# Encoder block on one core: where the first splits of the down projection and of its last unit are written, and how the final norm is multiplied

## The chip, the cores and the metric

The kernel runs on 1 core of one Trainium2 chip. The metric is the device time of one execution in microseconds; the median of three executions of the kernel before is 2689.52 us (2682.81 to 2689.66). The profile is of one more execution.

## The reference

The program computes one encoder layer (512 tokens, 2048 features, two attention mixers, then a SwiGLU feed-forward network of 5632 hidden features) and a final RMS norm. Only the end of it matters here:

```python
h2 = rms_norm(x, norm2_w[l]) * (1.0 + sc2) + sh2
ff = (jax.nn.silu(h2 @ w_ffn_gate[l]) * (h2 @ w_ffn_up[l])) @ w_ffn_down[l]
x = x + g2 * ff
return rms_norm(x, final_w)
```

with `rms_norm(x, w) = x * rsqrt(mean(x*x) + eps) * w`. All is float32.

## The kernel before, in words

**Arithmetic.** A float32 matmul is made of three: every operand is split into a high part (`S.activation(hi, src, AF.Copy)`, line 144, on ScalarE, called ACT in the profile) and a low part (`V.tensor_sub(lo, src, hi)`, line 145, on VectorE, DVE), both of type float32r, and `mm3` (lines 152 to 154) issues high*high, high*low and low*high into one PSUM bank on TensorE (PE).

**Order.** The order of the instructions on each engine is fixed when the kernel is built. A scheduler takes them by their place in the program (blocks under `tc.high_priority()` first) and by when it believes them ready, and puts each behind those already placed on its engine or DMA queue. At run time an engine works its list in order and waits at an instruction whose semaphores have not come; what stands behind it waits too. The DMA queues are SP's (`nc.sync`, nearly all loads and stores), ACT's (`nc.scalar`) and POOL's (`nc.gpsimd`, GpSimd); the kernel before issues no DMA from POOL. Tiles are handed out of pools. Pools lie on two stacks (left and right); a new pool's tiles are placed by the scheduler only after the pools under which it lies have been released, in program order; at run time a tile waits only for the old tiles that it overlaps (`reuse_waits="tile"`).

**Buffers.** `raw_tile` gives one of 5 staging buffers of 512 KB (128 x 1024 f32), shared by weights (`raw`) and by features read back (`ffr`). `wtile` gives one of 5 pairs of split weight buffers (`whi`, `wlo`). PSUM has 8 banks: four tagged `mm`, two `S`, one `T`, one `Y`.

**Gate and up products.** For each of 11 units `n` (512 hidden features) `group7` makes the gate and the up product by a seven-product scheme: 4 steps of 84 matmuls over the normalised features `hx` (pools `f_x` left, `f3` right), on seven banks (`BANK`: four `mm`, two `S`, `Y`). `wforms` loads the weights of a step and builds two sums of blocks in the tiles `ta` (2 buffers) and `tb`. At the end lines 839 to 846, under high priority, combine the banks into a tile `c` (3 buffers, pool `c_p`, right). Then ACT takes SiLU of the gate's tile, DVE multiplies the two (line 914, two instructions) and a DMA stores the product to `ff_d[n]` in HBM (line 915): from SP, and for the last unit from ACT.

**Down projection.** `FF` gives the hidden features of units back: for each pair of two 128-feature slices it loads half of `ff_d[u]` (line 959) and splits it into tiles `f0h`, `f0l`, `f1h`, ... of pool `p_f`. `form2` runs 512 output columns: per step of two slices one `wsplit` of `w_down`, then for each slice 3 matmuls into each of four `mm` banks (one for each 128 tokens, index `i`), then `pump()`, which takes one item off the list `later`; at the end `residual` multiplies each bank by the gate row `g2` (line 725, DVE) and adds it to `x2` (line 726, here on POOL). Units 0 to 4 run first, for the four column blocks `cc`, then units 5 to 9. `later` holds `reload`: the loads of `g2` (four DMAs, 1 MB) and of the four 1 MB tiles `xr` (the residual stream `x2`), in pool `p_c`.

**Last unit.** Unit 10's features are split into pool `p_fl`; its weights (four column blocks, each in two halves `k`) are split into tiles `w0h`, `w0l` to `w3h`, `w3l` of pool `p_l`, which lies where `p_f` was. Then, for each 128 tokens `i` and each `cc`, 12 matmuls into an `mm` bank, `residual` on DVE with a square on ACT (line 241, with its sum), and after the fourth `cc` `row_rstd` (lines 245 and 230 to 236: seven small DVE instructions and a square root on ACT), and line 999, which multiplies four times in one instruction by the row factor and by `final_w` (`fw`), each followed by a store of 256 KB from SP.

Of the kernel before, what the change touches and what calls it, by code (L numbers as in the profile page):

```python
# [13 lines left out]
F32 = mybir.dt.float32  # L14
# [5 lines left out]
P = 128  # L20
D = 2048
# [76 lines left out]
def encoder_block(ctx: ExitStack, tc, xp, xT, c, w_ada, ada1_w, b_ada, norm1_w, w_in, q_norm_w, k_norm_w, tb,  # L98
# [24 lines left out]
    def raw_tile(name="raw"):  # L123
        return buffer("raw", [P, 1024], F32, wbufs["raw"], name)
# [6 lines left out]
    def bank(tag):  # L131
        return ps.tile([P, 512], F32, tag=tag, name=tag, bufs={"mm": 4, "S": 2, "T": 1, "Y": 1}[tag])
# [10 lines left out]
    def split(hi, lo, src, eng=V):  # L143
        S.activation(hi, src, AF.Copy)  # L144
        eng.tensor_sub(lo, src, hi)  # L145
# [63 lines left out]
    def form2(w, c0, xs, evac, r0=0, eng=V, tiles=range(NT)):  # L209

        n = len(xs)
        banks = {i: bank("mm") for i in tiles}
        for k0 in range(0, n, 2):
            m = min(2, n - k0)
            hi, lo = wsplit(w, r0 + k0, m, c0, 512, eng)
            for kk in range(m):
                xh, xl = xs[k0 + kk]
                for i in tiles:
                    sl = slice(i * P, (i + 1) * P)
                    mm3(banks[i], xh[:, sl], xl[:, sl], hi[:, kk], lo[:, kk], k0 + kk == 0, k0 + kk == n - 1)  # L220
            pump()
        for i in tiles:
            evac(i, banks[i])
# [125 lines left out]
    def rows(dst, src):  # L349
        for q in range(4):  # L350
            nc.sync.dma_start(dst[:, q * 512:(q + 1) * 512], src[q].partition_broadcast(P).rearrange("p o d -> p (o d)"))
# [406 lines left out]
    def form_pool(name, side):  # L758
        return tc.alloc_tile_pool(name=name, bufs=1, side=side, reuse_waits="tile")
# [62 lines left out]
    def group7(wsrc, xs, order, dst):  # L822

        bk = {r: bank(BANK[r]) for r in ORDER}
        for n, s in enumerate(order):
            w = wsrc(s)
            for r in ORDER:
                (wh, wl), (xh, xl) = w[r], xs[s][r]
                for q in range(2):
                    for c in range(2):  # L830
                        o = bk[r][:, c * 256:(c + 1) * 256]
                        cs = slice(c * P, (c + 1) * P)
                        first, last = n == 0 and q == 0 and c == 0, n == len(order) - 1 and q == 1
                        mm3(o, wh[:, q, cs], wl[:, q, cs], xh[:, q], xl[:, q], first, last, skip_group_check=True)
        p = {r: b.rearrange("p (c n) -> p c n", c=2) for r, b in bk.items()}
        (d11, d12), (d21, d22) = dst
        with tc.high_priority():
            p1 = io.tile([P, 512], F32, tag="io", name="p1").rearrange("p (c n) -> p c n", c=2)
            S.activation(p1, p[1], AF.Copy)
            V.tensor_add(d11, p[2], p1)  # L840
            V.tensor_add(d21, p[6], p1)
            V.tensor_add(d12, p[5], d21)
            V.tensor_add(d12, p[3], d12)
            V.tensor_add(d21, p[7], d21)
            V.tensor_add(d22, p[5], d21)
            V.tensor_sub(d21, d21, p[4])
# [48 lines left out]
    def c_tile():  # L895
        c = c_p.tile([P, 2048], F32, tag="c", name="c", bufs=3)
        return c, c.rearrange("p (a t q n) -> p a t q n", a=2, t=2, q=2)

    for n in range(FU):
        cs = []  # L900
        for w in (w_gate, w_up):
            c, v = c_tile()
            cs.append(c)
            if n == 0 and w is w_gate:
                for f in range(4):
                    S.activation(v[:, f // 2, :, f % 2], banks[f].rearrange("p (t n) -> p t n", t=2), AF.Silu)
                continue
            dst = (v[:, 0, 0], v[:, 1, 0]), (v[:, 0, 1], v[:, 1, 1])
            group7(lambda s: wforms(w, 4 * s, n * 512), hx, range(SU), dst)
            if w is w_gate:  # L910
                S.activation(c, c, AF.Silu)
        for a in range(2):
            sl = slice(a * 1024, (a + 1) * 1024)
            V.tensor_mul(cs[1][:, sl], cs[1][:, sl], cs[0][:, sl])
        (nc.sync if n < FU - 1 else nc.scalar).dma_start(ff_d[n], cs[1])
    c_p.release()
    f3.release()
    for p in f_x[::-1]:
        p.release()

    wbufs["at"] = 0


    def reload(i):
        if i == 0:
            x2[:] = [p_c.tile([P, D], F32, name=f"xr{i}") for i in range(NT)]
            rows(g2, g2_d)
        nc.sync.dma_start(x2[i], x2_d[:, i])

    p_c = form_pool("p_c", "right")  # L930
    g2 = p_c.tile([P, D], F32, name="g2")
    later.append(lambda: None)
    later.extend(functools.partial(reload, i) for i in range(NT))
    p_fl = form_pool("p_fl", "left")
    p_f = form_pool("p_f", "left")

    class Tokens:

        def __init__(self, t):
            self.t = t  # L940
# [4 lines left out]

    class FF:

        def __init__(self, pool, u0, n):
            self.pool, self.u0, self.n, self.pairs = pool, u0, n, {}

        def __len__(self):
            return 4 * self.n
# [1 line left out]
        def __getitem__(self, k):  # L954
            j, q = divmod(k, 2)
            if j not in self.pairs:
                n, a = divmod(j, 2)
                raw = raw_tile("ffr")
                nc.sync.dma_start(raw, ff_d[self.u0 + n][:, a * 1024:(a + 1) * 1024])
                hl = [self.pool.tile([P, 1024], F32R, tag=f"f{j}{t}", name=f"f{j}{t}") for t in "hl"]  # L960
                split(*hl, raw)
                self.pairs[j] = hl
# [6 lines left out]
    xs = FF(p_fl, 10, 1)  # L969
    xs = [xs[k] for k in range(4)]  # L970
    p_f.release()


    f0 = 40
# [4 lines left out]
    wl = []  # L979
    for cc in range(4):  # L980
        hi, lo = pair(p_l, f"w{cc}", 4 * 512, 1)
        for k in range(0, 4, 2):
            raw, _ = unit(w_down, f0 + k, 2, cc * 512, 512)
            sl = slice(k * 512, (k + 2) * 512)
            split(hi[:, sl], lo[:, sl], raw)
        wl.append((hi, lo))
    for i in range(NT):
        sl = slice(i * P, (i + 1) * P)
        for cc in range(4):
            b = bank("mm")  # L990
            hi, lo = wl[cc]
            for k in range(4):
                ks = slice(k * 512, (k + 1) * 512)
                mm3(b, xs[k][0][:, sl], xs[k][1][:, sl], hi[:, ks], lo[:, ks], k == 0, k == 3)
            residual(cc, g2, sq3, V)(i, b)
        r = row_rstd(sq3[i])
        for cc in range(4):
            cs = slice(cc * 512, (cc + 1) * 512)
            V.scalar_tensor_tensor(x2[i][:, cs], x2[i][:, cs], r, fw[:, cs], op0=ALU.mult, op1=ALU.mult)
            nc.sync.dma_start(out[i * P:(i + 1) * P, cs], x2[i][:, cs])  # L1000
    p_l.release()
    p_fl.release()
    p_c.release()
    wq.release()
    io.release()
    wp.release()
# [30 lines left out]
```

## Time and profile before

| | |
|---|---|
| median of 3 executions | 2689.52 us |
| the profiled execution's own time | 2689.41 us |
| its span, first to last instruction | 2687.6 us |
| granted TensorE clock, mean | 0.988 |
| DVE busy | 1777.6 us, 66% of the span |
| ACT busy | 956.5 us, 36% |
| DMA read from and written to HBM | 392.11 MB and 32.52 MB |
| up product of the last unit ends, on PE | about 2184.2 us |
| down projection begins, on PE | 2191.17 us |
| last unit begins, on PE | 2628.82 us |

Times in the rows are us from the start of the span unless marked ns. A timeline row gives start, duration, engine, line, operation, output <- inputs, shape and count, and in brackets how long the engine stood idle before it and what released it. A window row gives for each engine the busy time and the number of instructions, then the granted clock of TensorE, the share of the DMA engines and GB/s.

### The profile page before, as it was taken

The page shows a single profiled execution, that of the slowest core. Times are in us where ns is not written, and L with a number is a line of the kernel's source. Part 1 is how long each engine was busy: PE and PEld are TensorE (multiplying, and loading weights), DVE is VectorE, ACT ScalarE, POOL GpSimd, SP SyncE. Part 2 cuts the span into 40 slices and gives each one's busy share as a digit, 9 for nine tenths or more (in the row PEclk, how much of TensorE's full clock was granted, in tenths as well). Part 3 has the DMA queues.
Part 4 walks back from the last instruction along what each step waited for, and adds up shares of the span by engine and source line. Part 5 has one row for each costly group of instructions (what it writes and reads, how often), then busy time and mean ns, then how long its engine had stood idle before and what let it go on. Part 6 is the DMA issues. An engine that isn't in the chain of part 4 may idle for free.

```text
span 2687.6 us, 38688 instructions
## 1 busy us (share of the span) xinstructions
PE 2608.7 (97%) x15415; PEld 2296.6 (85%) x15415; DVE 1777.6 (66%) x2508; ACT 956.5 (36%) x1292; POOL 110.3 (4%) x92
## 2 busy tenths in 40 slices
PE   6999999999999999999889999999999989999998
PEld 5888887888887878788789999999999988888886
DVE  6995687456666676653668888888888863243227
ACT  2324264223333333323544444444444442132122
POOL 0000000000000000001100000000000000010001
PEclk9999999999999999999999999999999999999999
DMA  7873424665554877774244344433444464343332
GB/s 249 278 273 106 130 83 130 213 205 170 179 179 142 265 260 248 246 240 136 84 126 126 120 132 126 126 118 119 126 127 126 126 231 146 101 146 122 100 110 86
DMA packets 247460, 427.16 MB, mean 159 GB/s; under 512 B 15984, under 2 KB 102368, under 8 KB 244720
## 3 DMA queue, kind: packets, MB, share of 16 engines
q1 hardware_dynamic: 246944, 423.59, 49.3%
q8 instruction: 121, 1.98, 0.3%
q10 hardware_dynamic: 336, 1.11, 0.1%
q14 instruction: 59, 0.48, 0.1%
HBM read 392.11 MB, written 32.52 MB: 158 GB/s over the span
## 4 chain that ended last, share of the span: by engine, by line
PE 86%; DMA 5%; DVE 5%; ACT 2%; issue 2%; POOL 0%; SPq 0%; DVEq 0%; ACTq 0%
PE mm L154 20%; PE mm L153 20%; PE mm L152 20%; PE S L152 5%; PE S L153 5%; PE S L154 5%; DMA raw<-in_w_ada 2%; PE Y L152 2%; PE Y L153 2%; PE Y L154 2%; DVE acc L303 1%; DVE wlo L145 1%; DMA g<-sga 1%; PE T L152 1%; PE T L154 1%
## 5 line engine op out<-in xcount | busy, mean ns | idle before, releaser
L145 DVE TENSOR_TENSOR wlo<-raw,whi 128x1024 fp32r<-128x1024 f32 (+1 forms) x467 | 528.5, 1135 | 459.2 <-ACT whi L144 458.3
L144 ACT ACTIVATE whi<-raw 128x1024 fp32r<-128x1024 f32 (+1 forms) x467 | 456.5, 979 | 1024.9 <-PE mm L154 420.2
L303 DVE SCALAR_TENSOR_TENSOR acc<-raw,cact,acc 128x512 f32<-128x512 f32 (+2 forms) x338 | 264.2, 788 | 118.2 <-DMA raw<-in_w_ada 111.2
L145 DVE TENSOR_TENSOR wlo<-ta,whi 128x1024 fp32r<-128x1024 f32 x84 | 102.8, 1224 | 71.5 <-ACT whi L144 71.5
L144 ACT ACTIVATE whi<-ta 128x1024 fp32r<-128x1024 f32 x84 | 89.6, 1067 | 132.0 <-PE mm L153 132.0
L144 ACT ACTIVATE whi<-tb 128x1024 fp32r<-128x1024 f32 x84 | 89.8, 1069 | 123.8 <-PE S L153 123.8
L154 PE MATMUL mm<-x1h,wlo 128*128 128x256 f32 x400 | 110.1, 276 | 1.6 <-DVE wlo L145 1.6
L152 PE MATMUL mm<-x1h,whi 128*128 128x256 f32 x400 | 110.4, 276 | 0.0
L153 PE MATMUL mm<-x1l,whi 128*128 128x256 f32 x400 | 110.3, 276 | 0.0
L145 DVE TENSOR_TENSOR wlo<-tb,whi 128x1024 fp32r<-128x1024 f32 x84 | 102.6, 1222 | 6.1 <-ACT whi L144 3.1
L152 PE MATMUL mm<-x0h,whi 128*128 128x256 f32 x368 | 102.4, 280 | 3.5 <-ACT whi L144 3.5
L154 PE MATMUL mm<-x0h,wlo 128*128 128x256 f32 x368 | 103.1, 280 | 2.6 <-DVE wlo L145 2.6
L153 PE MATMUL mm<-x0l,whi 128*128 128x256 f32 x368 | 102.6, 279 | 0.0
L726 POOL TENSOR_TENSOR xr<-xr,ro 128x512 f32<-128x512 f32 x32 | 50.1, 1599 | 1224.9 <-DVE ro L725 1224.9
L152 PE MATMUL mm<-x3h,whi 128*128 128x256 f32 x336 | 92.7, 276 | 0.0
L153 PE MATMUL mm<-x3l,whi 128*128 128x256 f32 x336 | 92.7, 276 | 0.0
L154 PE MATMUL mm<-x3h,wlo 128*128 128x256 f32 x336 | 92.7, 276 | 0.0
L152 PE MATMUL mm<-x2h,whi 128*128 128x256 f32 x336 | 92.7, 276 | 0.0
L153 PE MATMUL mm<-x2l,whi 128*128 128x256 f32 x336 | 92.7, 276 | 0.0
L154 PE MATMUL mm<-x2h,wlo 128*128 128x256 f32 x336 | 92.7, 276 | 0.0
L152 PE MATMUL S<-x2h,whi 128*128 128x256 f32 x336 | 92.7, 276 | 0.0
L153 PE MATMUL S<-x2l,whi 128*128 128x256 f32 x336 | 92.7, 276 | 0.0
(1310 smaller groups left out, 7848.0 us busy)
## 6 DMA issues: line engine op xcount, KB each, us to landing
raw<-in_w_in SPq DMA_DIRECT2D x133, 512.0 KB
raw<-in_w_gate SPq DMA_DIRECT2D x88, 512.0 KB
raw<-in_w_up SPq DMA_DIRECT2D x88, 512.0 KB
raw<-in_w_down SPq DMA_DIRECT2D x88, 512.0 KB
raw<-in_ada_w SPq DMA_DIRECT2D x64, 512.0 KB
raw<-in_w_ada SPq DMA_DIRECT2D x128, 256.0 KB
raw<-in_w_ada SPq DMA_DIRECT2D x64, 512.0 KB
raw<-in_w_out SPq DMA_DIRECT2D x40, 512.0 KB
```

What stands on the lines that cost most here:

```text
L144: S.activation(hi, src, AF.Copy)
L145: eng.tensor_sub(lo, src, hi)
L152: nc.tensor.matmul(o, lh, rh, start=start, stop=False, **kw)
L153: nc.tensor.matmul(o, lh, rl, start=False, stop=False, **kw)
L154: nc.tensor.matmul(o, ll, rh, start=False, stop=stop, **kw)
L303: V.scalar_tensor_tensor(acc, part, cact[:, k:k + 1], acc, op0=ALU.mult, op1=ALU.add)
L726: eng.tensor_add(x2[i][:, cs], x2[i][:, cs], o)
```

## The change

Five things are done.

1. A helper `ff_pair` loads and splits a pair of features into given tiles. `first_pairs`, called once after the weights of the last step of the last up product have been issued, does so for pairs 0 and 1 of unit 0: pair 0 into two tiles of tag `ta` (both buffers), pair 1 into the halves of one `c` tile. Pair 0 is used from there for all four column blocks of units 0 to 4, pair 1 for the first one only (`del xs.pairs[1]`); from the second on it is loaded and split again into `p_f`.
2. The store of the last unit's product goes from POOL's queue in place of ACT's.
3. The release of the feature pools, the new pools and the entries of `later` move into `down_pools`, called at the third pair (step `k0=4`) of the first `form2`, so that the reloads of `g2` and `xr` stand two steps later in the program.
4. The weights of the last unit's first two column blocks are loaded and split by `last_weights` into the `whi`/`wlo` buffers, ahead of the last `residual` of units 5 to 9; those of blocks 2 and 3 stay in `p_l`. The matmuls of the first 128 tokens go to banks `S`, `S`, `T`, `Y`.
5. `final_w` is multiplied into `x2` (DVE) right behind each residual; after `row_rstd` two of the four parts are multiplied by the row factor on DVE and two on ACT, and the latter are stored from ACT's queue.

```diff
+    early = {}
+    def ff_pair(unit_, a, hl):
+        raw = raw_tile("ffr")
+        nc.sync.dma_start(raw, ff_d[unit_][:, a * 1024:(a + 1) * 1024])
+        split(*hl, raw)
+        return hl
+    def first_pairs():
+        early[0] = ff_pair(0, 0, [wq.tile([P, 1024], F32R, tag="ta", name=f"e0{t}", bufs=2) for t in "hl"])
+        e1 = c_p.tile([P, 2048], F32R, tag="c", name="e1", bufs=3)
+        early[1] = ff_pair(0, 1, [e1[:, :1024], e1[:, 1024:]])
...
-            group7(lambda s: wforms(w, 4 * s, n * 512), hx, range(SU), dst)
+            def wsrc(s):
+                d = wforms(w, 4 * s, n * 512)
+                if s == SU - 1 and n == FU - 1 and w is w_up:
+                    first_pairs()
+                return d
+            group7(wsrc, hx, range(SU), dst)
...
-        (nc.sync if n < FU - 1 else nc.scalar).dma_start(ff_d[n], cs[1])
-    c_p.release()
-    f3.release()
-    for p in f_x[::-1]:
-        p.release()
+        (nc.sync if n < FU - 1 else nc.gpsimd).dma_start(ff_d[n], cs[1])
...
+    def down_pools():
+        c_p.release()
+        f3.release()
+        for p in f_x[::-1]:
+            p.release()
+        down["c"] = form_pool("p_c", "right")
+        down["g2"] = down["c"].tile([P, D], F32, name="g2")
+        later.append(lambda: None)
+        later.extend(functools.partial(reload, i) for i in range(NT))
+        down["fl"] = form_pool("p_fl", "left")
+        down["f"] = form_pool("p_f", "left")
...
             if j not in self.pairs:
+                if not down:
+                    down_pools()
                 n, a = divmod(j, 2)
...
+    def last_weights():
+        for cc in range(2):
+            us = [wsplit(w_down, f0 + k, 2, cc * 512, 512) for k in range(0, 4, 2)]
+            wl[cc] = [(hi[:, e], lo[:, e]) for hi, lo in us for e in range(2)]
     for u0 in (0, 5):
-        xs = FF(p_f, u0, 5)
+        xs = FF("f", u0, 5, early if u0 == 0 else None)
         for cc in range(4):
-            form2(w_down, cc * 512, xs, lambda i, b: residual(cc, g2, None, G)(i, b), r0=4 * u0)
+            ending = u0 == 5 and cc == 3
+            def evac(i, b):
+                if ending and i == 0:
+                    last_weights()
+                residual(cc, down["g2"], None, G)(i, b)
+            form2(w_down, cc * 512, xs, evac, r0=4 * u0)
+            if u0 == 0 and cc == 0:
+                del xs.pairs[1]
...
-    for cc in range(4):
+    for cc in range(2, 4):
         hi, lo = pair(p_l, f"w{cc}", 4 * 512, 1)
...
         for cc in range(4):
-            b = bank("mm")
+            b = bank("mm" if i else "SSTY"[cc])
...
-            residual(cc, g2, sq3, V)(i, b)
+            residual(cc, down["g2"], sq3, V)(i, b)
+            cs = slice(cc * 512, (cc + 1) * 512)
+            V.tensor_mul(x2[i][:, cs], x2[i][:, cs], fw[:, cs])
         r = row_rstd(sq3[i])
         for cc in range(4):
             cs = slice(cc * 512, (cc + 1) * 512)
-            V.scalar_tensor_tensor(x2[i][:, cs], x2[i][:, cs], r, fw[:, cs], op0=ALU.mult, op1=ALU.mult)
-            nc.sync.dma_start(out[i * P:(i + 1) * P, cs], x2[i][:, cs])
+            if cc % 2:
+                S.activation(x2[i][:, cs], x2[i][:, cs], AF.Copy, scale=r)
+            else:
+                V.tensor_scalar(x2[i][:, cs], x2[i][:, cs], r, None, op0=ALU.mult)
+            (nc.scalar if cc % 2 else nc.sync).dma_start(out[i * P:(i + 1) * P, cs], x2[i][:, cs])
```

More of the change, by code (lines that the diff above doesn't have):

```diff
@@ L914, in encoder_block @@
             V.tensor_mul(cs[1][:, sl], cs[1][:, sl], cs[0][:, sl])
-        (nc.sync if n < FU - 1 else nc.scalar).dma_start(ff_d[n], cs[1])
-    c_p.release()
-    f3.release()
-    for p in f_x[::-1]:
-        p.release()
-    wbufs["at"] = 0
+        (nc.sync if n < FU - 1 else nc.gpsimd).dma_start(ff_d[n], cs[1])
+    wbufs["at"] = 0
+    down = {}
+    def down_pools():
[9 more added lines that the diff above has]
+        down["f"] = form_pool("p_f", "left")
     def reload(i):
         if i == 0:
-            x2[:] = [p_c.tile([P, D], F32, name=f"xr{i}") for i in range(NT)]
-            rows(g2, g2_d)
+            x2[:] = [down["c"].tile([P, D], F32, name=f"xr{i}") for i in range(NT)]
+            rows(down["g2"], g2_d)
         nc.sync.dma_start(x2[i], x2_d[:, i])
[L930 to L935, printed above, removed]
     class Tokens:
@@ L946, in encoder_block, with __init__ @@
     class FF:
-        def __init__(self, pool, u0, n):
-            self.pool, self.u0, self.n, self.pairs = pool, u0, n, {}
+        def __init__(self, pool, u0, n, pairs=None):
+            self.pool, self.u0, self.n, self.pairs = pool, u0, n, pairs or {}
         def __len__(self):
@@ L956, in __getitem__ @@
             if j not in self.pairs:
+                if not down:
+                    down_pools()
                 n, a = divmod(j, 2)
[L958 to L962, printed above, removed]
-            return tuple(Tokens(half(t)[:, :, q]) for t in self.pairs[j])
+                self.pairs[j] = ff_pair(self.u0 + n, a, [down[self.pool].tile([P, 1024], F32R, tag=f"f{j}{t}",
+                                                                             name=f"f{j}{t}") for t in "hl"])
+            return tuple(Tokens(half(t)[:, :, q]) for t in self.pairs[j])
+    f0 = 40
+    wl = {}
+    def last_weights():
+        for cc in range(2):
+            us = [wsplit(w_down, f0 + k, 2, cc * 512, 512) for k in range(0, 4, 2)]
+            wl[cc] = [(hi[:, e], lo[:, e]) for hi, lo in us for e in range(2)]
     for u0 in (0, 5):
-        xs = FF(p_f, u0, 5)
+        xs = FF("f", u0, 5, early if u0 == 0 else None)
         for cc in range(4):
-            form2(w_down, cc * 512, xs, lambda i, b: residual(cc, g2, None, G)(i, b), r0=4 * u0)
-    xs = FF(p_fl, 10, 1)
+            ending = u0 == 5 and cc == 3
[6 more added lines that the diff above has]
+                del xs.pairs[1]
+    xs = FF("fl", 10, 1)
     xs = [xs[k] for k in range(4)]
-    p_f.release()
-    f0 = 40
+    down["f"].release()
     sq3 = [small.tile([P, 4], F32, tag=f"sq{i}", name=f"sq3{i}", bufs=1) for i in range(NT)]
@@ L985, in encoder_block @@
             split(hi[:, sl], lo[:, sl], raw)
-        wl.append((hi, lo))
+        wl[cc] = [tuple(t[:, k * 512:(k + 1) * 512] for t in (hi, lo)) for k in range(4)]
     for i in range(NT):
@@ L998, in encoder_block @@
             cs = slice(cc * 512, (cc + 1) * 512)
[L999 to L1000 removed]
+            if cc % 2:
[3 more added lines that the diff above has]
+            (nc.scalar if cc % 2 else nc.sync).dma_start(out[i * P:(i + 1) * P, cs], x2[i][:, cs])
     p_l.release()
[L1002 to L1003 removed]
+    down["fl"].release()
+    down["c"].release()
     wq.release()
```

5 lines of the change are left out of this document (1 added, 4 removed).

## The prediction

> **What bounds the kernel now.** I read the page's first part, then the waits of PE, then windows and engine timelines at the two places where PE stops.
>
> ```profile
> PE 2608.7 (97%) x15415; PEld 2296.6 (85%) x15415; DVE 1777.6 (66%) x2508; ACT 956.5 (36%) x1292; POOL 110.3 (4%) x92
> ```
>
> PE is busy 97% of the span, so the change can win only where PE stands idle or runs slowly, and behind its last matmul. Of the waits from 1900 us on, PE has two:
>
> ```profile
> PE mm L152 <- ACT f0h L144: 6.9, 1, 6.9
> PE mm L153 <- DVE w0l L145: 2.5, 2, 2.3
> ```
>
> The first is the start of the down projection, the second that of the last unit. The windows there and around:
>
> ```profile
> 2184.20:2191.17 6.97, 0.03 (x2) 0.00 (x1) 5.29 (x8) 1.11 (x2) 0.00 (x0) 0.84 0.32 100
> 2191.17:2196.40 5.23, 5.19 (x13) 3.67 (x14) 5.23 (x5) 3.74 (x4) 0.00 (x0) 0.56 0.99 338
> 2196.40:2248.00 51.60, 51.60 (x229) 42.74 (x228) 20.61 (x19) 15.95 (x15) 0.99 (x1) 1.00 0.78 288
> ...
> 2628.80:2645.20 16.40, 13.88 (x52) 10.19 (x51) 16.29 (x16) 4.42 (x7) 5.97 (x4) 0.90 0.33 97
> 2645.20:2656.10 10.90, 10.90 (x50) 9.02 (x49) 8.65 (x20) 4.39 (x10) 0.00 (x0) 1.00 0.19 67
> 2656.10:2667.00 10.90, 10.90 (x50) 9.03 (x49) 9.31 (x21) 3.09 (x10) 0.00 (x0) 1.00 0.34 120
> ```
>
> After each stop the granted clock is low (0.56 for 5.2 us; 0.90 over the first 16.4 us of the last unit); in between PE is full. The later tiles of the last unit run at PE's own pace, 10.90 us each, with DVE busy 8.65 to 9.31 us of it. Why PE stops first:
>
> ```profile
> 2182.29 1.06 ACT L144 ACTIVATE whi<-raw 128x1024 fp32r<-128x1024 f32 x1 [2.52 <-DVE c L841]
> 2189.63 0.38 ACTq L915 DMA_DIRECT2D ffd<-c  x1
> 2190.06 1.06 ACT L144 ACTIVATE f0h<-ffr 128x1024 fp32r<-128x1024 f32 x1 [6.70 <-DVE c L914]
> ```
> ```profile
> 2183.95 0.28 PE L154 MATMUL Y<-x1h,wlo 128*128 128x256 f32 x1
> 2191.17 0.79 PE L152 MATMUL mm<-whi,f0h 128*128 128x512 f32 x1 [6.94 <-ACT f0h L144]
> ...
> 2196.34 0.39 PE L152 MATMUL mm<-whi,f0h 128*128 128x512 f32 x1
> ```
>
> ACT's list has the store of the last unit's product ahead of the split of `f0`. The store waits for the multiplication at line 914, the split waits behind it, and PE for the split.
>
> **1. First features early: what goes.** The 6.94 us of idle. And the slow start: the 12 matmuls of slice 0 took 2196.34 - 2191.17 = 5.17 us. The full pace comes from these two rows, 22 matmuls apart:
>
> ```profile
> 2623.83 0.39 PE L154 MATMUL mm<-whi,f9l 128*128 128x512 f32 x1
> 2628.82 0.39 PE L152 MATMUL mm<-w0h,f0h 128*128 128x512 f32 x1
> ```
>
> 4.99 / 22 = 0.2268 us each, 2.72 us per slice, 5.44 us per step. So 2.45 us more; together **9.4 us**.
>
> What it adds ahead of the stop is two loads, two ACT splits of 1.06 us and two DVE splits of 1.22 us. The rows that bound them:
>
> ```profile
> 2170.29 1.23 DVE L145 TENSOR_TENSOR wlo<-ta,whi 128x1024 fp32r<-128x1024 f32 x1 [1.50 <-ACT whi L144]
> ...
> 2184.53 0.68 DVE L843 TENSOR_TENSOR c<-mm,c 128x512 f32<-128x512 f32 x1
> ...
> 2185.85 0.69 DVE L845 TENSOR_TENSOR c<-mm,c 128x512 f32<-128x512 f32 x1
> ...
> 2187.25 2.35 DVE L914 TENSOR_TENSOR c<-c 128x1024 f32<-128x1024 f32 x2
> ```
>
> The second `ta` buffer is free when its last reader ends at 2171.5; 12.5 us remain to 2184.1, in which DVE waits at gaps like the 1.50 us shown. ACT and DVE hide the splits under the last `group7`; without that cover they would cost 2 x 2.3 us. What is late next is the banks: `form2` needs the third and fourth `mm` bank 1.36 and 2.04 us after its start, at 2185.4 and 2186.1, and lines 843 and 845 let them go at 2185.2 and 2186.5. Cost 0.4 us if DVE's list stays, 0 if the weight split ahead of line 843 comes earlier, up to 1.6 if one 1.22 us split is put in between. I take **0.3** (range 0 to 1.6), since those lines have priority.
>
> **2 and 3. The store from POOL, and the moved reloads.** POOL has no instruction in the first two windows, so nothing queues behind the store's wait for line 914. Its data are read only by unit 10's load, eight column blocks later: nothing. No row shows a DMA from POOL. By the Trainium skill, "DMA: Bandwidth & Descriptors", section "Anatomy of one DMA — SWDGE (gpsimd) path", 2.0 us plus bytes over 436 GB/s, an estimate of 4.4 us for this 1 MB; by it the sum stays, as nothing on PE's path waits for the store.
>
> The reloads are different: PE now asks for everything 9.1 us sooner, while `g2` may wait longer.
>
> ```profile
> SPq L351 <- DVE c L914: 4.6, 1, 4.6
> ```
> ```profile
> 2189.68 3.41 SPq L351 DMA_DIRECT2D g<-g2d  x4
> ```
> ```profile
> 2206.98 1.06 ACT L144 ACTIVATE whi<-raw 128x1024 fp32r<-128x1024 f32 x1 [12.07 <-DMA raw<-in_w_down]
> ```
>
> `g2` lies on `c` tiles (it waits for line 914). `e1` is such a tile, read until step 2 ends: 2184.2 + 10.9 = 2195.1, so the reloads may start 5.4 us later than now, and all behind them on SP too. Now the fifth weight unit comes out of this queue 17.3 us after `g2`'s issue. After the change units 5, 6 and 7 are needed at 2206.0, 2211.4 and 2216.8. What speaks for no wait: now the five staging buffers hold five feature pairs that ACT can't split before 2190; then pairs 0 and 1 are split by about 2173 and two buffers turn to weights, and the reloads stand two steps later in the program, so units 5 and 6 go ahead of them. If unit 6 is behind after all: 2195.1 + 17.3 + 2.4 (its splits) = 2214.8, 3.4 us late, and 2.45 for the slow clock: 5.9. I take **0** (0 to 5.9). The second load of pair 1, in the second column block, is hidden by PE's matmuls, since even in the first block (third window) ACT was busy for 15.95 and DVE for 20.61 of 51.60 us; it costs nothing.
>
> **4. Last unit's weights early: what goes.**
>
> ```profile
> 2602.79 1.99 ACT L144 ACTIVATE w0h<-raw 128x1024 fp32r<-128x1024 f32 x2
> ```
> ```profile
> 2627.05 2.78 DVE L725 TENSOR_TENSOR ro<-mm,g 128x512 f32<-128x512 f32 x4 [22.91 <-PE mm L154]
> 2629.75 3.89 DVE L145 TENSOR_TENSOR w0l<-raw,w0h 128x1024 fp32r<-128x1024 f32 x2
> ```
> ```profile
> 2676.94 0.39 PE L154 MATMUL mm<-w3h,f1l 128*128 128x512 f32 x1
> ```
>
> `w0h` is made 24 us early, but `w0l` stands on DVE behind the four residuals, which wait for PE, while DVE idles 22.91 us. From 2628.82 to the last matmul's start at 2676.94 are 48.12 us; 191 steps of 0.2268 make 43.3. So **4.8 us** can go: 2.53 of waits, 2.27 of slow clock. Four weight units in the rotating buffers are split one per 5.44 us as PE frees them, the last about 2625.9, ahead of the residuals. The waits here are worth a look against the Trainium skill, "TensorE: Matmul & The Clock Gate", section "What's actually happening": the clock falls after an idle window of about 3.4 us. Here stops of 2.3 and 0.3 us were enough (window 0.90), so the row decides; by the page only 2.5 us of the 4.8 would be owed to the wait, and the rest would stay.
>
> Blocks 2 and 3 keep the old path: their four low splits stay behind the residuals.
>
> ```profile
> L145 DVE TENSOR_TENSOR w0l<-raw,w0h 128x1024 fp32r<-128x1024 f32 x2 | 3.9, 1984 | 0.0
> L726 DVE TENSOR_TENSOR xr<-xr,ro 128x512 f32<-128x512 f32 x16 | 11.1, 692 | 0.4
> L999 DVE SCALAR_TENSOR_TENSOR xr<-xr,rr,fw 128x512 f32<-128x512 f32 x16 | 11.0, 748 | 0.1
> ```
> ```profile
> L745 DVE TENSOR_SCALAR n<-x,rr x2: 481/482/482, 1292.1 to 1311.8; 128x512 f32<-128x512 f32 x2
> ```
>
> Two at 1.98 (POOL adds meanwhile) and two at about 1.4 end near 2636.4; PE wants them from 2634.3, half by half, and they come in time; but the first block's residual, ready at 2631.5, starts 4.9 us late. Per tile DVE trades four of 748 ns for four of 692 (priced as line 726) and two of 482 (line 745): +0.74, so 9.4 to 10.05 of 10.90, and catches up 0.85 to 1.5 us per tile, 2.6 to 4.5 in three. I take a lag of **1.0** at the end (0 to 4.9). The new banks for tile 0 only give PE more room.
>
> **5. The tail.**
>
> ```profile
> 2677.44 0.69 DVE L725 TENSOR_TENSOR ro<-mm,g 128x512 f32<-128x512 f32 x1 [0.69 <-PE mm L154]
> 2678.16 0.69 DVE L726 TENSOR_TENSOR xr<-xr,ro 128x512 f32<-128x512 f32 x1
> 2679.70 0.16 DVE L245 TENSOR_REDUCE ssq<-sq 128x1 f32<-128x4 f32 x1 [0.85 <-ACT junk L241]
> ...
> 2681.29 2.74 DVE L999 SCALAR_TENSOR_TENSOR xr<-xr,rr,fw 128x512 f32<-128x512 f32 x4
> ```
> ```profile
> 2678.95 0.63 ACT L241 ACTIVATE junk<-xr 128x512 f32<-128x512 f32 x1 [1.38 <-DVE xr L726]
> ```
> ```profile
> 1291.26 0.73 ACT L741 ACTIVATE n<-x,rr 128x512 f32<-128x512 f32 x1
> ```
>
> The product with `fw` can start when the square has read its input, at 2679.6, just ahead of the reduction: +0.5 (0 to 0.7). The 2.74 us become two of 0.48 on DVE beside two of 0.73 on ACT, with a store's issue of 0.38 perhaps in between: 1.4 (to 1.8). The last store's flight stays. Net **-0.85** (-1.5 to 0).
>
> **Sum.** 9.4 - 0.3 - 0 + 4.8 - 1.0 + 0.85 = 13.75 us off the profiled execution's 2689.41 us (span 2687.6 plus 1.8 around it): **2675.7 us**. The median is 0.11 above that execution; one run of three was 6.7 us below, so a median can come out lower by chance.
>
> **Rivals.**
> *A, the reloads stop PE.* As worked out, 5.9 us: 2681.6. For it: SP works in order and `g2` waits for `e1`. Against: the freed staging buffers.
> *B, DVE sets the last unit.* The product with `fw` must wait for the square. If DVE's list has it right behind, a block takes 0.72 + 0.79 + 0.63 + 0.69 = 2.83 us, a tile 4 x 2.83 + 1.59 (2679.70 to 2681.29) + 0.9 = 13.8. From 2636.4, four tiles end at 2691.6, then 3.5 for the last store (2687.6 less line 999's end, 2684.0): 7.5 later than now, less 9.1 from the start of the down projection: 2687.8. With half the waits filled 12.3 per tile: 2681.8. Against: a scheduler that sees a backlog has other residuals to put in the gaps.
> *C, the first pairs are not early.* If their splits still stand behind something late, only 4.65 us are left: 2684.8. Against: their tiles are free by 2171.5 and their source is old.
> *D, slower.* The tile of `f2` is placed only after `e1`'s last reader, so its split can stand on ACT behind a weight split whose load stands on SP behind the reloads. Then `f2` comes at 2195.1 + 17.3 + 3.3 = 2215.7, where PE wants it at 2195.1: 20.6 us, and 2.45 of slow clock, 23 against 13.75 won: 2698.7. It decides from a stop of 11.3 us on (that load landing after about 2203). For it: exactly this queueing behind an early-placed instruction makes today's 6.94 us. Against: the units ahead should be loaded by then.
>
> **How the numbers follow.** Forecast 0.63 (own range 2671.5 to 2679.5), A 0.10, B 0.14, C 0.05, D 0.08. A measurement of this kernel tells 0.3% from no change, 8.1 us: faster is below 2681.4, slower above 2697.6. Faster: all of the forecast, 0.06 of A, 0.03 of B: 0.72. Slower: 0.06 of D. The same: 0.22. The range 2671 to 2684 takes the forecast, A and half of B: 0.80. Its low end is the sum without any cost (9.4 + 4.8 + 1.5, 2673.7) less 2.7 for the lower runs.
>
> **What would show it.** Right: the first matmul of `f`'s successors at once behind the last `group7`, granted clock 1.0 there, no ACT wait for line 914; no wait on `w0l`'s successors; last unit in about 43.3 us; line 725's last wait on PE, not a backlog. Wrong: an idle PE at step 3 or later of the first `form2` behind an `ffr` or weight load (A, D); DVE busy without PE as releaser to the end, or DVE waiting on ACT's square (B); ACT or DVE splits of pair 0 after 2184 (C).

## The result, and the profile after

| | before | after |
|---|---|---|
| median (20 executions each) | 2686.24 us (2679.62 to 2717.66) | 2672.85 us (2669.14 to 2706.05) |
| ratio after / before | | 0.9953 (95% 0.993 to 0.9975) |
| profiled execution, its span | 2689.41, 2687.6 us | 2670.28, 2668.5 us |
| granted TensorE clock, mean | 0.988 | 0.991 |

The changed kernel is 13.4 us faster by the medians; 2675.7 was predicted, with 13.75 us off. Two of the 20 executions of either kernel take some 30 us longer, and the ratio counts them.

The two profiled executions differ by more, 19.1 us, and not all of that is the change. The start of the last matmul of the gate/up projections is a mark up to which both programs do the same work. The timeline of PE in the changed kernel (start, duration, engine, line, operation, output <- inputs) at that mark, at the first `f2`, at the first matmul of the last unit and at the last matmul:

```profile
2177.95 0.28 PE L154 MATMUL Y<-x1h,wlo 128*128 128x256 f32 x1
2178.06 0.40 PE L152 MATMUL mm<-whi,e0h 128*128 128x512 f32 x1
...
2189.05 0.39 PE L152 MATMUL mm<-whi,f2h 128*128 128x512 f32 x1
...
2613.37 0.39 PE L152 MATMUL S<-whi,f0h 128*128 128x512 f32 x1
...
2656.66 0.39 PE L154 MATMUL mm<-w3h,f1l 128*128 128x512 f32 x1
```

The mark stands at 2177.95, before the change at 2183.95: 6.00 us arise ahead of everything that was changed, and between executions of all kernels here it lies anywhere from 2176.0 to 2186.0. So the work behind it is compared in three stretches: from the mark to the first matmul of the last unit (435.42 us, before 444.87), from there to the start of the last matmul (43.29, before 48.12), and from there to the end of the span (11.84, before 10.66). The differences are -9.45, -4.83 and +1.18: 13.10 us, which with the 6.00 make up the 19.1.

PE and its clock, page part 1, then windows at the two places where PE stood before (PE, PEld, DVE, ACT and POOL busy, granted clock, DMA share, GB/s):

```profile
PE 2599.4 (97%) x15415; PEld 2291.2 (86%) x15415; DVE 1780.8 (67%) x2517; ACT 962.0 (36%) x1301; POOL 110.4 (4%) x93
```
```profile
2178.06:2183.60 5.54, 5.54 (x26) 4.44 (x25) 5.50 (x8) 1.06 (x1) 0.00 (x0) 1.00 0.64 208
...
2613.30:2624.25 10.95, 10.95 (x51) 9.04 (x49) 10.62 (x10) 2.73 (x4) 6.09 (x4) 1.00 0.29 111
...
2635.13:2646.00 10.87, 10.87 (x49) 9.01 (x48) 10.13 (x24) 5.03 (x13) 0.00 (x0) 1.00 0.29 98
```

PE is full and the clock 1.00 at both places. Before, PE stood idle for 6.94 us at the first, with a clock of 0.56 behind that, and the last unit began with 0.90. No matmul behind the mark waits for anything. The 48 matmuls from 2178.06 to 2189.05 take 10.99 us where 48 x 0.2268 make 10.89, so the banks cost 0.1 us at most. DVE is busy for 10.62 and 10.13 us of the two tiles of the last unit, near its limit, and PE still runs on.

How the first features came early, and what held the reloads, by the timelines of ACT, DVE, POOL and SP, then the waits (sum, count, longest) and the DMA issues (KB, us from issue to landing):

```profile
2156.39 1.05 ACT L144 ACTIVATE e0h<-ffr 128x1024 fp32r<-128x1024 f32 x1
```
```profile
2165.55 1.23 DVE L145 TENSOR_TENSOR e0l<-ffr,e0h 128x1024 fp32r<-128x1024 f32 x1
```
```profile
2184.37 0.70 POOL L935 DMA_DIRECT2D ffd<-c  x1 [830.35 <-DVE c L934]
```
```profile
2188.90 1.76 SPq L351 DMA_DIRECT2D g<-g2d  x4
```
```profile
SPq L351 <- DMA ffd<-c: 2.3, 1, 2.3
```
```profile
ffd<-c POOLq DMA_DIRECT2D x1, 1024.0 KB, 4.5
```

Pair 0 is whole 11 us ahead of PE's demand. POOL waits alone for the product (line 934) and then stores. The store lands 4.5 us after its issue, and one thing does wait for that: `g2`, for 2.3 us, as it lies on the tile that the store reads.

The tail is the part that got longer. DVE at the end of the changed kernel:

```profile
2657.26 0.68 DVE L725 TENSOR_TENSOR ro<-mm,g 128x512 f32<-128x512 f32 x1
2658.13 0.69 DVE L1030 TENSOR_TENSOR xr<-xr,fw 128x512 f32<-128x512 f32 x1 [0.19 <-ACT junk L241]
2658.74 0.68 DVE L726 TENSOR_TENSOR xr<-xr,ro 128x512 f32<-128x512 f32 x1
2660.21 0.69 DVE L1030 TENSOR_TENSOR xr<-xr,fw 128x512 f32<-128x512 f32 x1 [0.79 <-ACT junk L241]
2660.82 0.15 DVE L245 TENSOR_REDUCE ssq<-sq 128x1 f32<-128x4 f32 x1
```

The product of block 2 with `fw` (2658.13) stands between the two steps of the last residual, and the product of block 3 (2660.21) ahead of the reduction. The reduction starts 4.16 us after the last matmul's start; before it was 2679.70 - 2676.94 = 2.76. From the reduction to the end it is 7.68 us, before 7.90. So the two-factor norm loses 1.40 us on one side of the reduction and wins 0.22 on the other. Why it wins so little is seen in SP's queue, first the changed kernel, then the one before:

```profile
2662.91 0.81 SPq L1038 DMA_DIRECT2D out<-xr  x2
```
```profile
2682.07 2.32 SPq L1000 DMA_DIRECT2D out<-xr  x4
```

From the first store's issue to the end are 2668.5 - 2662.91 = 5.59 us, before 2687.6 - 2682.07 = 5.53. The arithmetic behind it is shorter by more than 1 us, and the time is the same. Windows of one microsecond show the reason, first of the changed kernel, then of the one before:

```profile
2664.00:2665.00 1.00, 0.00 (x0) 0.00 (x0) 0.00 (x0) 0.00 (x0) 0.00 (x0) 0.50 1.07 391
2665.00:2666.00 1.00, 0.00 (x0) 0.00 (x0) 0.00 (x0) 0.00 (x0) 0.00 (x0) 0.50 1.04 356
```
```profile
2683.00:2684.00 1.00, 0.00 (x0) 0.00 (x0) 1.00 (x2) 0.00 (x0) 0.00 (x0) 0.50 1.02 391
```

The DMA engines are full, at up to 391 GB/s in both. At that rate 256 KB take 0.67 us, and line 999 made 256 KB in 2.74 / 4 = 0.69: the four stores were already bound by their transfer. What is won, 0.22 us, is about what the first store comes earlier: it is issued 2.09 us behind the start of the reduction, before 2.37.

### The profile page after: what moved, and what is told of

Its sections match the earlier page's. It is cut to its first block, busy times and chain, and to the rows that moved or that the text cites. A ratio compares the mean times of both kernels' runs of the same rounds, so it can differ in the third digit from the quotient of the medians.

```text
span 2668.5 us, 38695 instructions
## 1 busy us (share of the span) xinstructions
PE 2599.4 (97%) x15415; PEld 2291.2 (86%) x15415; DVE 1780.8 (67%) x2517; ACT 962.0 (36%) x1301; POOL 110.4 (4%) x93
## 4 chain that ended last, share of the span: by engine, by line
PE 90%; DVE 5%; DMA 2%; issue 1%; ACT 1%; POOL 0%; SPq 0%; DVEq 0%; ACTq 0%
PE mm L154 21%; PE mm L153 21%; PE mm L152 21%; PE S L152 5%; PE S L153 5%; PE S L154 5%; PE Y L152 2%; PE Y L153 2%; PE Y L154 2%; DVE acc L303 1%; DMA raw<-in_w_ada 1%; DVE wlo L145 1%; PE T L152 1%; PE T L153 1%; PE T L154 1%
## 5 line engine op out<-in xcount | busy, mean ns | idle before, releaser
L154 PE MATMUL Y<-x1h,wlo 128*128 128x256 f32 x336 | 92.7, 276 | 0.0
```

Source lines behind the costliest of these rows:

```text
L154: nc.tensor.matmul(o, ll, rh, start=False, stop=stop, **kw)
```

## The experiments

Theory: the three parts act in three separate stretches and add up; the gain at the start needs both the early pairs and the store's move; the tail's loss is the product with `fw` in DVE's order. The rivals are with each run. Stretches in us as defined above, from each kernel's timeline of PE; "stops" are PE's waits in them.

| kernel | first | last unit | tail | stops of PE |
|---|---|---|---|---|
| before | 444.87 | 48.12 | 10.66 | 6.94; 2.26, 0.27 |
| after | 435.42 | 43.29 | 11.84 | none |
| e1_store_only | 444.10 | 48.20 | 10.79 | 0.76, 5.71; 2.26, 0.47 |
| e2_early_only | 435.94 | 48.03 | 10.76 | 0.21; 2.26, 0.57, 0.58 |
| e3_weights_only | 445.24 | 43.30 | 10.70 | 7.83 |
| e5_norm_only | 445.03 | 48.03 | 11.41 | 7.54; 2.26 |
| e4_old_norm | 435.48 | 43.29 | 10.71 | none |
| e11_mixed_norm | 435.40 | 43.29 | 11.22 | none |
| e12_changed_again | 435.39 | 43.29 | 11.84 | none |
| e9_reload_twice | 447.84 | 43.29 | 11.94 | 2.68, 5.39 |
| e6_store_on_act | 440.77 | 43.30 | 11.68 | 3.46 |
| e10_stores_on_sp | 435.38 | 43.29 | 12.93 | none |

The first four experiments ran on one chip beside the kernel before (2691.17 us there), the next four on a second one (2687.93), the last two on a third (2686.6).

**e1, the store alone.** The kernel before with one word changed.

```diff
-        (nc.sync if n < FU - 1 else nc.scalar).dma_start(ff_d[n], cs[1])
+        (nc.sync if n < FU - 1 else nc.gpsimd).dma_start(ff_d[n], cs[1])
```

> Only the store of the last unit's product moves from ACT's queue to POOL's; every other list stays as before. First stretch (last matmul of the gate and up products to first matmul of the last unit, 444.87 us before). Theory 1, ACT's list was not the only one: the split of f0's low part also stands on DVE behind line 914, so f0h starts near 2183.4 on that time scale but f0l only near 2189.7 instead of 2191.15; PE's third matmul waits for it, and the stretch gets 1 to 2 us shorter, with the slow clock still there. Theory 2, the store on ACT was the whole cause: PE goes on near 2186, the stretch gets 5 to 8 us shorter. Theory 3, the split waits for the release of the old pools: nothing.

Measured 2686.89 us, ratio 0.997 (0.9938 to 1.0001); the first stretch is 0.77 us shorter. PE's two stops there:

```profile
2177.95 0.50 PE L152 MATMUL mm<-whi,f0h 128*128 128x512 f32 x1 [0.76 <-ACT f0h L144]
...
2184.39 0.79 PE L154 MATMUL mm<-whi,f0l 128*128 128x512 f32 x1 [5.71 <-DVE f0l L145]
```
```profile
2180.84 2.36 DVE L914 TENSOR_TENSOR c<-c 128x1024 f32<-128x1024 f32 x2
2183.11 1.22 DVE L145 TENSOR_TENSOR f0l<-ffr,f0h 128x1024 fp32r<-128x1024 f32 x1
```

`f0h` is there at once now, but `f0l` stands on DVE behind the multiplication at line 914, and PE stops at its first use instead. The stop moved from ACT's list to DVE's. The store on ACT was not the whole cause.

**e2, parts 1 to 3 of the change alone:** early pairs, store on POOL, moved reloads; weights, banks and norm as before.

> Parts 1 to 3 alone (early pairs, store from POOL, moved reloads); the last unit and the norm as before. Additive theory: first stretch 444.87 to 435.4 us (9.4 shorter), last unit 48.1 us and tail 10.7 us as before; time 9.4 us below the kernel before. Rival, the parts need each other (the moved reloads or the second load of pair 1 cost something that part 4 hides): less than 8 us.

Measured 2680.49 us, ratio 0.9953 (0.9914 to 0.9991). The first stretch is 8.93 us shorter, 0.21 us of the missing half microsecond being one wait on a residual at about 2400. The first stop is gone. The last unit takes as long as before, but its window is not the same:

```profile
2618.00:2629.00 11.00, 7.59 (x31) 5.34 (x30) 10.93 (x10) 1.91 (x2) 5.97 (x4) 1.00 0.45 142
```

The granted clock is 1.00 here, behind the same first stop of 2.26 us, and PE makes longer stops after it (0.57 and 0.58 us, before 0.27) in place of running slowly. So it is the late low splits on DVE that set the time of the last unit, with the low clock or without it.

**e3, part 4 alone:** `last_weights`, its call ahead of the last residuals, and the banks, on the kernel before.

```diff
+                if ending and i == 0:
+                    last_weights()
...
-            b = bank("mm")
+            b = bank("mm" if i else "SSTY"[cc])
```

> Part 4 alone (first two weight blocks of the last unit split early, banks S, S, T, Y for the first tile); norm as before. Theory 1: last unit 48.1 to 43.3 us, and DVE, with 8.7 to 9.3 us of work per tile of 10.9, catches up with its late start, so the tail stays at 10.7: time 4.8 us below before. Theory 2, the late start (four low splits behind the residuals) lasts to the end whatever the norm: tail 11.5 or more, time only about 4 us below.

Measured 2684.08 us, ratio 0.9949 (0.990 to 0.9998). The last unit takes 43.30 us, the tail is as before, and the first stop stays (7.83 us).

**e5, part 5 alone:** the product with `fw` behind each residual and the halves on DVE and ACT, on the kernel before.

> Part 5 alone (final norm in two factors, half of it and its stores on ACT). Theory 1, the product with final_w stands between a tile's sums and their reduction: first stretch 444.9 and last unit 48.1 us as before, tail 11.8 us or more instead of 10.7, time 1 to 3 us above before. Theory 2, the tail's loss in the changed kernel came from the late start of DVE alone: tail 9.5 to 10.2 us, time 0.5 to 1 us below before.

Measured 2688.42 us, ratio 0.9972 (0.9936 to 1.0007). The time cannot tell it from the kernel before; the tail can, 11.41 against 10.66 us, where theory 1 had 11.8 or more. DVE there:

```profile
2679.52 0.69 DVE L725 TENSOR_TENSOR ro<-mm,g 128x512 f32<-128x512 f32 x1
2680.19 0.69 DVE L997 TENSOR_TENSOR xr<-xr,fw 128x512 f32<-128x512 f32 x1
...
2682.27 0.69 DVE L997 TENSOR_TENSOR xr<-xr,fw 128x512 f32<-128x512 f32 x1 [0.79 <-ACT junk L241]
2682.88 0.15 DVE L245 TENSOR_REDUCE ssq<-sq 128x1 f32<-128x4 f32 x1
```

The last matmul starts at 2679.09, so the reduction comes 3.79 us later (2.76 before): the loss needs no part of the change but the norm. It is 0.37 us less than in the changed kernel: the last residual starts 0.43 and not 0.60 us after the last matmul, and the product of block 2 behind it need not wait 0.19 for ACT's square.

**e4, the change without part 5.**

```diff
-            V.tensor_mul(x2[i][:, cs], x2[i][:, cs], fw[:, cs])
...
-            if cc % 2:
-                S.activation(x2[i][:, cs], x2[i][:, cs], AF.Copy, scale=r)
-            else:
-                V.tensor_scalar(x2[i][:, cs], x2[i][:, cs], r, None, op0=ALU.mult)
-            (nc.scalar if cc % 2 else nc.sync).dma_start(out[i * P:(i + 1) * P, cs], x2[i][:, cs])
+            V.scalar_tensor_tensor(x2[i][:, cs], x2[i][:, cs], r, fw[:, cs], op0=ALU.mult, op1=ALU.mult)
+            nc.sync.dma_start(out[i * P:(i + 1) * P, cs], x2[i][:, cs])
```

> The changed kernel with the norm of before (one instruction with both factors, all stores from SP). Theory 1, the two-factor norm costs the tail 1.2 us: first stretch 435.4 to 436, last unit 43.3, tail 10.7 us instead of 11.84: 1.1 us below the changed kernel, 14 below before. Theory 2, the tail's loss came from PE ending earlier while DVE still has the late splits: tail 11.5 to 12 as in the changed kernel.

Measured 2672.94 us, ratio 0.9943 (0.9896 to 0.9989), tail 10.71. With the rest of the change in place, the old norm gives the old tail back:

```profile
2655.29 0.69 DVE L725 TENSOR_TENSOR ro<-mm,g 128x512 f32<-128x512 f32 x1 [0.64 <-PE mm L154]
2656.01 0.69 DVE L726 TENSOR_TENSOR xr<-xr,ro 128x512 f32<-128x512 f32 x1
2657.55 0.16 DVE L245 TENSOR_REDUCE ssq<-sq 128x1 f32<-128x4 f32 x1 [0.85 <-ACT junk L241]
```

DVE waits for PE again at the last residual, and no product stands between the residual and the reduction. By the stretches this is the fastest of the kernels run.

**e11, a mixed norm.** On e4, for the last 128 tokens only, blocks 0 and 1 are multiplied by `fw` early and by the row factor late (one on DVE, one on ACT); blocks 2 and 3 keep line 999's form.

```diff
+            if i == NT - 1 and cc < 2:
+                cs = slice(cc * 512, (cc + 1) * 512)
+                V.tensor_mul(x2[i][:, cs], x2[i][:, cs], fw[:, cs])
```

> As the run with the old norm, but in the last tile blocks 0 and 1 take final_w early and afterwards the row factor on DVE (block 0) and ACT (block 1, stored from ACT's queue); blocks 2 and 3 as before in one DVE instruction. If the four last stores are bound by their transfer, which begins with the first of them, the tail gets as much shorter as the first store comes earlier, 0.2 to 0.3 us: 10.4. If the last arithmetic bounds it, 0.7 to 1 us: 9.7 to 10.0.

Measured 2672.26 us, ratio 0.9936 (0.9901 to 0.9971), tail 11.22 where 10.4 was expected: a miss. DVE:

```profile
2658.86 0.69 DVE L1031 TENSOR_TENSOR xr<-xr,fw 128x512 f32<-128x512 f32 x1 [0.25 <-ACT junk L241]
2659.47 0.68 DVE L726 TENSOR_TENSOR xr<-xr,ro 128x512 f32<-128x512 f32 x1
2660.07 0.68 DVE L725 TENSOR_TENSOR ro<-mm,g 128x512 f32<-128x512 f32 x1
...
2662.33 0.16 DVE L245 TENSOR_REDUCE ssq<-sq 128x1 f32<-128x4 f32 x1 [0.85 <-ACT junk L241]
```

The last matmul starts at 2658.88. Block 1's product runs just then, so block 3's first step starts 1.19 us after it instead of 0.50. Even a product two blocks ahead reaches the end. From the reduction to the end it is 7.77 us against 7.95 in e4: these 0.18 us are near the 0.2 to 0.3 of the theory that the transfer bounds the stores, and the miss lies ahead of the reduction.

**e12, the changed kernel again,** beside e4 and e11.

> The changed kernel once more, beside the two above on one chip. If the three stretches are the program's own and the rest is scatter between executions: 435.4 to 436, 43.3 and 11.8 us again, whatever the time before the last gate and up product (2178 us in the first profile, 2184 in that of the kernel before).

Measured 2677.08 us, ratio 0.9977 (0.9935 to 1.0019); stretches 435.39, 43.29 and 11.84, within 0.03 of the first profile. The interval of the ratio is wider than the effect sought, and those of e4, e11 and e12 overlap. That e4 is 1.1 us faster is read from the stretches alone.

**e9, reloads doubled.** On the changed kernel each `x2` reload is issued twice, to price rival A's queue. The edit does more than double the bytes: the second load goes into the same tile as the first.

```diff
-        nc.sync.dma_start(x2[i], x2_d[:, i])
+        for _ in range(2):
+            nc.sync.dma_start(x2[i], x2_d[:, i])
```

> The changed kernel with each 1 MB reload of x2 issued twice (4 MB more on SP's queue). In the changed kernel f6's low part was ready at 2207.9, PE wanted it at 2210.8: a margin of 2.9 us. Theory A, the queue is in order and bound by transfer at some 0.42 MB/us: 3 MB more ahead of f6 are 7.2 us, so PE stops 4 to 5 us, runs slowly after it (up to 2.4), and the first stretch grows by 4 to 8 us. Rival, small loads pass the large ones on the 16 engines or the cover is wider: below 1 us.

Measured 2684.32 us (one execution); the first stretch is 12.4 us longer than in the changed kernel, where 4 to 8 were expected. SP's queue, its waits for `xr` (sum, count, longest), and the split of pair 6 on ACT:

```profile
2192.23 11.18 SPq L957 DMA_DIRECT2D xr<-x2d  x5
2203.51 0.48 SPq L903 DMA_DIRECT2D ffr<-ffd  x1
2204.04 12.72 SPq L957 DMA_DIRECT2D xr<-x2d  x3
```
```profile
SPq L957 <- DMA xr<-x2d: 20.4, 4, 7.7
```
```profile
2213.99 1.06 ACT L144 ACTIVATE f6h<-ffr 128x1024 fp32r<-128x1024 f32 x1 [20.68 <-DMA ffr<-ffd]
```

The 11.18 and 12.72 us of the merged rows are mostly waits: SP waits four times, 20.4 us in all, for a load of `xr` to land, each time ahead of the second load into the same tile. The loads behind them start late: `f6h` comes at 2214, and PE stops twice. So what stands on SP behind the reloads can stop PE, as rival A has it, and with one reload each it does not. What more bytes alone would cost is not shown, since these waits are the edit's own. How near it is, by the changed kernel's last low split of pair 6:

```profile
2206.63 1.23 DVE L145 TENSOR_TENSOR f6l<-ffr,f6h 128x1024 fp32r<-128x1024 f32 x1 [13.53 <-ACT f6h L144]
```

It ends at 2207.86; PE comes to pair 6 four steps after the first `f2`, at 2189.05 + 4 x 5.44 = 2210.8. The margin is 2.9 us.

**e6, the store on ACT** with early pairs: the changed kernel with only the store moved back. The order of ACT's list changed with it: a second weight split came to stand ahead of `f2h`.

```diff
-        (nc.sync if n < FU - 1 else nc.gpsimd).dma_start(ff_d[n], cs[1])
+        (nc.sync if n < FU - 1 else nc.scalar).dma_start(ff_d[n], cs[1])
```

> The changed kernel with the store of the last unit's product back on ACT's queue. Theory 1, with the first pairs split ahead, nothing that PE needs soon stands behind the store (its wait ends at line 934's end, 6 us after the last gate and up matmul; pair 2 is wanted 11 us after it): first stretch 435.4 to 435.9 as in the changed kernel. Rival, the queue matters as much as the early split: a stop of 1 us or more at pair 2 or at a weight unit, stretch 437 or more.

Measured 2683.35 us (one execution); the first stretch is 5.35 us longer than in the changed kernel, so theory 1 did not hold. ACT, DVE, PE, SP and a window there:

```profile
2191.58 1.06 ACT L144 ACTIVATE whi<-raw 128x1024 fp32r<-128x1024 f32 x1 [4.57 <-PE mm L154]
2191.89 0.36 ACTq L935 DMA_DIRECT2D ffd<-c  x1
2198.39 1.06 ACT L144 ACTIVATE whi<-raw 128x1024 fp32r<-128x1024 f32 x1 [5.75 <-DMA raw<-in_w_down]
2199.36 1.04 ACT L144 ACTIVATE f2h<-ffr 128x1024 fp32r<-128x1024 f32 x1
```
```profile
2192.68 1.23 DVE L145 TENSOR_TENSOR wlo<-raw,whi 128x1024 fp32r<-128x1024 f32 x1 [0.81 <-ACT whi L144]
```
```profile
2200.45 0.50 PE L152 MATMUL mm<-whi,f2h 128*128 128x512 f32 x1 [3.46 <-ACT f2h L144]
```
```profile
2193.93 0.37 SPq L159 DMA_DIRECT2D raw<-in_w_down  x1
```
```profile
2200.00:2206.00 6.00, 5.55 (x17) 4.46 (x18) 5.25 (x5) 3.24 (x4) 0.00 (x0) 0.72 1.00 361
```

The store holds nothing up: it goes out at 2191.89, while ACT works on the weight split that waited for PE, as in the changed kernel. What `f2h` waits for is the second weight split: its load is issued by SP only at 2193.93, when the low split on DVE that ends at 2193.90 has freed the staging buffer, and `f2h` stands behind it on ACT. PE stops at pair 2 for 3.46 us and runs at a granted clock of 0.72 for the 6 us that follow. So the theory was right about the store itself, and wrong in taking the order of ACT's list as given: moving the store moved another instruction. This is rival D's queue in small, features behind a late weight split on ACT, though that split's load is late for its buffer and not for the reloads.

**e10, all stores from SP.** The changed kernel with the ACT half of the stores on SP.

```diff
-            (nc.scalar if cc % 2 else nc.sync).dma_start(out[i * P:(i + 1) * P, cs], x2[i][:, cs])
+            nc.sync.dma_start(out[i * P:(i + 1) * P, cs], x2[i][:, cs])
```

> The changed kernel with all stores of the output on SP's queue. Theory 1, the last four stores are bound by their transfer: tail 11.6 to 12.0 us, as with two queues (11.84). Rival, the issues in one queue set the end: tail longer by 0.5 us or more. The build moves some of DVE's residuals too, so a shift of DVE's lag of some tenths may come with it.

Measured 2675.49 us (one execution), tail 12.93, 1.09 longer than the changed kernel's, where theory 1 had 11.6 to 12.0. DVE:

```profile
2662.36 0.68 DVE L725 TENSOR_TENSOR ro<-mm,g 128x512 f32<-128x512 f32 x1
...
2666.04 0.15 DVE L245 TENSOR_REDUCE ssq<-sq 128x1 f32<-128x4 f32 x1
```

The last matmul starts at 2660.77: the reduction comes 5.27 us after it (4.16 in the changed kernel), since the order of the residuals on DVE came out differently. From the reduction to the end it is 2673.7 - 2666.04 = 7.66 us against 7.68: which engine issues the stores makes no difference here, and the rival's number is met for another reason than its own. That is also what the Trainium skill says ("DMA: Bandwidth & Descriptors", section "Issuing engines are not separate DMA queues"): transfers from any engine share the same DMA engines, and issuing from several saves only issue time.

## Why the prediction was right, and which term was off

**The start of the down projection.** Predicted 9.4 less 0.3 for the banks, 9.1; measured 9.45, the banks 0.1 at most. The mechanism was right: the stop and the slow start behind it both went. What the prediction did not see is how much hangs on the order of the lists. The store's move was costed at nothing, and was nothing as a cost. As a gain it is worth 0.77 us by itself (e1), since line 914 stands ahead of `f0`'s low split on DVE as the store does ahead of the high split on ACT; the prediction showed the row of line 914 and named only the store. With the early pairs in place, the kernel with the store on ACT is 5.35 us slower (e6), not because anything waits behind the store but because the list of ACT came out in another order.

**The reloads.** Predicted 0, measured 0. The reason given, that the staging buffers free early, was not tested by itself, and no run leaves out part 3 by itself. One detail was wrong: "nothing on PE's path waits for the store", and of its readers only unit 10's load was named. `g2` waits for the store's landing, 4.5 us after its issue; the fit of the Trainium skill ("DMA: Bandwidth & Descriptors", section "Anatomy of one DMA — SWDGE (gpsimd) path") makes an estimate of 4.4 for it. PE reads `e1`, on which `g2` lies too, until the first `f2` at 2189.05 anyway, so it costs nothing here. The margin to rival A is 2.9 us.

**The last unit.** Predicted 4.8, measured 4.83, and 4.82 in e3 alone. The split of it into 2.53 us of waits and 2.27 of slow clock did not hold. In e2 the clock is 1.00 and the last unit takes 48.03 us all the same, because PE then waits longer for the low splits of blocks 0 and 1 (stops of 2.26, 0.57 and 0.58). The late low splits alone cost 4.74 us there; in the kernel before the low clock fell into time that PE would have waited. The sum came out because part 4 takes these splits off the path, whichever way the loss is divided.

**The tail.** Predicted a lag of 1.0 and a gain of 0.85, together 0.15 longer; measured 1.18 longer. The mis-sized step is: "The 2.74 us become two of 0.48 on DVE beside two of 0.73 on ACT, with a store's issue of 0.38 perhaps in between: 1.4 (to 1.8). The last store's flight stays." That is 1.35 us won; 0.22 was measured. The stores come out one every 0.69 us before, which is the time their transfer takes, so the last flight does not stay: it queues behind the other three. The sum of the terms ahead of the reduction, 1.0 + 0.5, comes close to the 1.40 measured, but by luck. The lag of 1.0 was to come from the late start of DVE; with part 4 and the old norm the tail is 10.70 (e3) and 10.71 (e4), so there is no lag. In the changed kernel too the last residual starts only 0.1 us later after the last matmul (0.60 against 0.50). Instead, two products stand in the last chain: block 2's makes line 726 start 1.48 us after line 725 (0.72 before), block 3's makes the reduction start 2.08 after line 726 (1.54 before); 0.10 + 0.76 + 0.54 are the 1.40. Only the last of these was in the prediction, with 0.5. Rival B's mechanism, a product that waits for ACT's square, is seen at both, but PE was never held by it and the price is 1.4 us and not 7.5.

**The rivals.** C did not occur: pair 0 was split by 2166.8. D did not occur in the changed kernel; e6 shows its queue with a stop of 3.46 us. That e2's, e3's and e5's stretches each return the changed kernel's or the kernel before's to within 0.55 us shows that the parts add across the stretches.

**The sum.** 13.75 predicted, 13.10 by the stretches, 13.4 by the medians. The 0.65 us missing are the tail's 1.03, less 0.35 more at the start and 0.03 in the last unit.

## What to carry to other kernels

When a stop has two instructions queued ahead of its operand on two engines, taking away one only moves the stop to the other: look for the second before pricing the first. A store moved to another queue can change the order of an engine's other work, so read the list of the built kernel before giving the store the credit (e6). At the end of a kernel, compare the pace at which the last results are made with the pace at which their stores move; if these are equal, faster arithmetic wins only what the first store comes earlier, and any instruction put ahead of the final reduction to get it is a plain loss. Of such a change keep the parts that remove stops and leave the tail as it was (e4), and judge parts of a microsecond by stretches between two marks, as executions here scatter by up to 10 us ahead of the marks.

## What was not expected of the hardware

A stop of PE in the first stretch costs about 2 us beyond itself, whatever its length from 3.5 to 7.8 us. Against the changed kernel's 435.42 us that stretch shows: 6.94 us of stop and 2.51 more (before), 7.83 and 1.99 (e3), 7.54 and 2.07 (e5), 3.46 and 1.89 (e6), two stops of 8.07 together and 4.35 more (e9), that is 2.2 each; in e1 stops of 0.76 and 5.71 cost 2.21 more together, no more than one stop does. The windows behind the stops show why: a granted clock of 0.56 over 5.23 us before, which is an estimate of 2.3 us lost, and of 0.72 over 6 us in e6, 1.7 us. Removing a stop of 3.46 us is thus worth 5.35, one of 7.83 us 9.82.

For shorter stops the runs do not agree. The same stop of 2.26 us at the start of the last unit is followed by a low clock in the kernel before (0.90 over 16.4 us) and by a full one in e2 (1.00 over 11 us); why is open. What the low clock costs also depends on what PE would have done with the time: here it would have waited, and the last unit takes 48.12 and 48.03 us.
